# Order of the rest copies, the place of the low-rank load, the length of a warm-up bridge and the turn of the output operands in a one-core encoder block

## The chip, the cores and the metric

The kernel runs on one core of a Trainium2 chip. It is measured by the device time of one execution in microseconds (us). Three runs of the kernel before took 904.07, 904.47 and 905.79 us, with a median of 904.47. One further execution was recorded by the profiler.

## The reference

One encoder layer on 512 tokens of width 2048 in float32. A conditioning vector gives shift, scale and gate; the normalised and modulated input h is projected to all inputs of two mixers, dilated window attention (16 heads of 64, three patterns) and gated linear attention (GLA, 4 heads, whose decay comes from a low-rank product). Both results are gated, joined and projected out.

```python
    mod = jax.nn.silu(c) @ w_cond[layer] + b_cond[layer]
    shift, scale, gate = jnp.split(mod, 3, axis=-1)
    h = rms_norm(x) * (1.0 + scale[:, None]) + shift[:, None]
    proj = h @ w_in[layer]
    aq, ak, av, ag, gq, gk, gv, gg, lr_f, lr_b = jnp.split(proj, PROJ_SPLITS, axis=-1)
    ...
        o_p, lse_p = dilated_window_attention(aq, ak, av, rel_bias, window, dilation)
    ...
    mix_w = jax.nn.softmax(jnp.stack(lses, axis=0), axis=0)
    att = jnp.einsum('pbsh,pbshe->bshe', mix_w.astype(av.dtype), jnp.stack(outs, axis=0))
    a_out = att.reshape(B, S, ATT_WIDTH) * jax.nn.silu(ag)
    ...
    log_g_f = (jax.nn.log_sigmoid((lr_f @ gla_gate_up_fwd[layer] + gla_gate_bias_fwd[layer]).astype(jnp.float32))
               / GLA_GATE_NORM).reshape(ks_)
    ...
    o_bwd = jnp.flip(gla_chunked(jnp.flip(gq, 1), jnp.flip(gk, 1), jnp.flip(gv, 1),
                                 jnp.flip(log_g_b, 1)), 1)
    g_o = rms_norm(o_fwd + o_bwd).reshape(B, S, GLA_WIDTH) * gla_norm_gain[layer]
    g_out = g_o * jax.nn.silu(gg)
    y = jnp.concatenate([a_out, g_out], axis=-1) @ w_out[layer]
    x = x + gate[:, None] * y
return rms_norm(x) * final_gain
```

## The kernel before

Every large product keeps float32 accuracy by splitting both sides into a high and a low part: three() (L229) issues high by high, low by high and high by low, three matmuls of 512 columns. Weights arrive by DMA as raw tiles of 512 KB; ScalarE (ACT) copies the high part (split_hi, L493), VectorE (DVE) subtracts it to leave the low part (split_lo, L477). Each of the two takes about a microsecond and works a few groups ahead of the matmuls.

The stages follow one another on TensorE (PE), whose order is the order of the program text. First come the conditioning row, the normalisation and the first projections (sta and stb, up to about 96 us). Then the units qk2, qk4, qk6 and gk, each of 64 ticks; a tick is one three(). Attention runs beside these four units, four heads in each, from about 200 to 444 us: a side item, such as the scores of a tile, has a place between 0 and 1 of its unit and is put in at that tick. Then comes the V unit with 112 ticks, which makes the GLA values by seven Strassen products, with the low-rank product at ticks 9 to 24 and GLA head 0 beside it. The units ag0, ag1, gg0 and gg1 make the gates. Last, from about 744 us, stands the output product: seven Strassen products (in the order P1, P7, P6, P4, P5, P3, P2) for each of two pairs of row blocks, four weight groups (O0 to O55) per product, each group 12 matmuls of PE or about 2.7 us. The tail after PE's last matmul normalises and stores.

On the other engines and on the DMA queue of SyncE (SP) a scheduler orders the instructions from the place at which they were written and from what they need; each engine and each queue then runs strictly in that order, so an instruction that waits holds up what stands behind it. In a few marked regions the text's own order holds.

**Bridge.** At the start PE has nothing to multiply until the first activations are normalised. warm(n) (L293) issues n products of a constant tile hot into a bank that nobody reads: five at the very start, then, after the products that spread the conditioning row (L299), six more (L324).

**Attention of one head.** Scores s (L839, L840) for four query tiles go through a bias with a running sum on DVE (L847, in parts of 160 and 256 columns), an exponential on ACT (L851), a reciprocal on DVE (L854) and a scaling on GpSimd (POOL, L864). PE transposes the probabilities to t (L882); ACT copies the high part to pth (L888), DVE subtracts to leave ptl (L889). What is left of the first tile, one 128 x 128 block r, is transposed once (L899) and spread over four places of the two tiles by rest(): four copies of 32 x 128 on ACT (L906) and four subtractions on DVE (L908), in two pairs: two copies, their two subtractions, then the other two of each. The value product o (L915, L917) then needs all of pth and ptl. S in the orders below is a partial sum for the Strassen operands, made on the side.

**Low rank.** lrb, 256 KB of low-rank weights, is loaded on SP's queue after the gk unit has been written (L1303), in the same ring of tiles as other work; ACT and DVE split it to lrs (L1306, L1307), used by low_rank at tick 9 of V. upr (loaded at L1320) is split to ups at place 0.2 of V.

**GLA head 0.** GLA_FIRST (L122) gives the places of ten items in the V unit; the eighth and ninth, outs(0) and outs(1), are the products go (L1123), which need the decay-masked scores at (L1106, L1108 on DVE).

**Output operands.** Each Strassen product has its own operand made of blocks of cat (the joined mixer results): A11, S3, S2, A22, S1, S4 and A12, in halves z = 0 and 1. to_s1 (L1471), to_s2 (L1474) and to_s4 (L1477) form sums in place on DVE, 1.2 us each; halves() splits into a high (ACT, L1458) and a low tile (DVE, L1459). P6 uses S2, P4 uses A22, P5 uses S1 and P3 uses S4. These makings hang on a list by pair, product and group (later), and product() issues them when it writes that group, right after the lower split of the group's first weight tile; the last to_s1 and to_s2 stand before the output product, after the eviction of gg1 (L1202).

Of the kernel before, what the change touches and what calls it, by code (L numbers as in the profile page):

```python
# [10 lines left out]
F32 = mybir.dt.float32  # L11
# [109 lines left out]
GLA_AT = (0.01, 0.02, 0.33, 0.46, 0.46, 0.56, 0.64, 0.76, 0.76, 0.88)  # L121
GLA_FIRST = (0.3, 0.38, 0.55, 0.62, 0.775, 0.81, 0.86, 0.9, 0.92, 0.97)  # L122

# [68 lines left out]
def block_kernel(ctx: ExitStack, tc: tile.TileContext, a: dict):  # L192
# [108 lines left out]
    with tc.manual_schedule(engines=PLANNED):  # L301
# [18 lines left out]
        for j in range(4):  # L320
            spread(j, ch, True)
            spread(j, cl, False)
            act(sb[:, 512 * j:512 * j + 512], pcs[j], AF.Silu)
        warm(6)  # L324

# [492 lines left out]
    def attention(pairs):  # L818
# [77 lines left out]
        def rest(h):  # L896

            pk = PJ(f"r{h}")
            nc.tensor.transpose(pk[:, :P], pr_.pop((h, 0))[:, 0:128], ident)  # L899
            hi, lo = pts  # L900
            to = [(hi, 0, hi, 32), (hi, 0, lo, 0), (hi, 96, lo, 96), (hi, 64, hi, 96)]
            parts = [(t[a:a + 32, REST_OF[i], :], u[b:b + 32, REST_OF[i], :], pk[96 - 32 * i:128 - 32 * i, :P])
                     for i, (t, a, u, b) in enumerate(to)]
            for pair in (parts[:2], parts[2:]):
                for up, _, of in pair:
                    act(up, of, AF.Copy)  # L906
                for up, low_, of in pair:
                    tt(low_, of, up.bitcast(F32), op=ALU.subtract)  # L908

# [383 lines left out]

    ps = unit("gk", False, attention((6, 7)))
    kp_.close()
# [5 lines left out]

    lrb = T2("lrb")
    nc.sync.dma_start(lrb.rearrange("p (k c) -> p k c", k=KT), a["w_lr"][0])  # L1303
    lrs = gp.tile([P, KT, 2, 32], F32R, tag="g", name="lrs")
    lrb3 = lrb.rearrange("p (k c) -> p k c", k=KT)
    act(lrs[:, :, 0, :], lrb3, AF.Copy)  # L1306
# [176 lines left out]
    gate_evict(ps, cat[3], "g1")  # L1483
    to_s1(1)
    to_s2(1)
    mid.close()
# [147 lines left out]
    def later(pair, prod, g, go):  # L1634
        todo.setdefault((pair, prod, g), []).append(go)

    def product(pair, prod, ps, first, last, rows=(0, 1)):

# [25 lines left out]
    def a12():  # L1664
        operand("A12", [B8(f"A12{e}", [4, 512], F32R) for e in "hl"])

    for z in range(2):
        later(0, "P1", 2 * z, halves("S2", z, part(z, 0)))
        later(0, "P7", 2 * z, halves("A22", z, part(2 + z, 1)))
        later(0, "P6", 2 * z, halves("S1", z, part(z, 1)))  # L1670
        later(0, "P6", 2 * z + 1, lambda z=z: (to_s4(z), halves("S4", z, part(z, 0))()))
    later(0, "P4", 0, a12)
# [135 lines left out]
```

## Time and profile before

| | |
|---|---|
| runs | 904.07, 904.47, 905.79 us |
| profiled execution, its own time | 907.22 us |
| its span in the trace | 905.4 us |
| ACT, busy share | 54% |
| POOL, busy share | 14% |
| mean DMA rate | 268 GB/s |
| HBM read, written | 224.64 MB, 51.47 MB |

A profile row of the timeline has the start from the span's beginning in us, the duration, the engine, the source line, the operation, written tile <- read tiles, its shape and count, and in brackets the idle time ahead of it with what ended it. PEld are weight loads, which lie beside PE's matmuls; a row of PE ends later than the next begins, as matmuls are pipelined, so the distance between starts says more than the durations. SPq rows are DMA issues. The groups that the change touches, from the list of the costliest groups (busy us, mean ns of one, idle time ahead and its main releaser behind the bars):

```profile
L888 ACT ACTIVATE pth<-t 128x384 fp32r<-128x384 f32 x64 | 31.0, 485 | 19.8 <-PE t L882 11.1
L889 DVE TENSOR_TENSOR ptl<-t,pth 128x384 fp32r<-128x384 f32 x64 | 35.2, 551 | 5.2 <-ACT pth L888 3.7
L906 ACT ACTIVATE pth<-r 32x128 fp32r<-32x128 f32 x64 | 17.2, 269 | 9.9 <-PE r L899 4.5
L915 PE MATMUL o<-pth,vv 128*128 128x512 f32 (+1 forms) x64 | 15.9, 369 | 2.2 <-DVE pth L908 1.1
```

### The profile page before, as it was taken

What the parts mean: (1) busy time and instruction counts of PE and PEld (TensorE: products, weight loads), DVE (VectorE), ACT (ScalarE), POOL (GpSimd) and SP (SyncE); (2) the same over time, 40 slices, a digit from 0 to 9 for tenths busy, and PEclk for the clock granted to TensorE, in tenths of its full rate; (3) what the DMA queues carried; (4) which work ended last, traced back from release to release, by engine and by line L of the source; (5) the groups of instructions that cost most, each with busy time, mean ns of one, the idle gap of its engine ahead of it and who ended that gap; (6) DMA issues with size and microseconds to landing.
All of it is one profiled execution on the core that took longest, in us unless ns stands there. A gap on an engine that the chain in (4) does not pass through costs nothing.

```text
span 905.4 us, 12339 instructions
## 1 busy us (share of the span) xinstructions
PE 890.0 (98%) x4159; PEld 739.2 (82%) x4159; DVE 731.2 (81%) x1220; ACT 491.6 (54%) x841; POOL 125.9 (14%) x219
## 2 busy tenths in 40 slices
PE   8999999999999999999999999999999999999996
PEld 6888788888888888887778888888888888888885
DVE  7998799878989989888568668595787559797687
ACT  5554533466655745655657554373664248455454
POOL 0000000023323333243000101112020100000001
PEclk9999999999999999999999999999999999999999
DMA  9999489398798898998778879778796988777863
GB/s 342 401 411 363 186 344 367 134 306 226 202 266 273 247 265 247 249 298 223 232 260 255 311 206 308 206 249 262 231 279 208 275 286 289 282 288 249 289 238 154
DMA packets 65547, 242.33 MB, mean 268 GB/s; under 512 B 9190, under 2 KB 11526, under 8 KB 55883
## 3 DMA queue, kind: packets, MB, share of 16 engines
q1 hardware_dynamic: 58724, 199.23, 61.5%
q0 software_dynamic: 6464, 42.01, 19.4%
q8 instruction: 33, 0.54, 0.2%
q10 hardware_dynamic: 296, 0.30, 0.1%
q14 instruction: 30, 0.25, 0.1%
HBM read 224.64 MB, written 51.47 MB: 305 GB/s over the span
## 4 chain that ended last, share of the span: by engine, by line
PE 91%; DVE 3%; ACT 2%; DMA 2%; issue 1%; SPq 0%; DVEq 0%; ACTq 0%
PE ps_qk L230 5%; PE ps_qk L232 5%; PE ps_qk L231 5%; PE g L232 4%; PE g L230 4%; PE g L231 4%; PE stb L232 3%; PE stb L231 3%; PE stb L230 3%; PE ps_ag L232 3%; PE ps_ag L230 3%; PE ps_ag L231 3%; PE o L915 3%; PE sta L230 3%; PE sta L231 3%; PE sta L232 3%
## 5 line engine op out<-in xcount | busy, mean ns | idle before, releaser
L864 POOL TENSOR_SCALAR p<-p,st 128x32 f32<-128x32 f32 (+2 forms) x108 | 59.8, 565 | 159.9 <-DVE st L854 91.2
L328 DVE CUSTOM_DVE_ANT_0 cb<-cb,sb,c_bcond 128x2048 f32<-128x2048 f32 (+1 forms) x32 | 73.4, 2295 | 1.9 <-DMA cb<-in_wm 1.6
L851 ACT ACTIVATE p<-p,st 128x416 f32<-128x416 f32 x64 | 41.0, 641 | 49.2 <-DVE st L847 42.3
L429 POOL DMA_DIRECT2D T<-in_w_o x32 | 23.2, 725 | 159.4 <-ACT V2h L493 14.8
L888 ACT ACTIVATE pth<-t 128x384 fp32r<-128x384 f32 x64 | 31.0, 485 | 19.8 <-PE t L882 11.1
L889 DVE TENSOR_TENSOR ptl<-t,pth 128x384 fp32r<-128x384 f32 x64 | 35.2, 551 | 5.2 <-ACT pth L888 3.7
L882 PE MATMUL t<-c_ident,p 128*128 128x128 f32 x192 | 31.3, 272 | 0.0
L882 PEld LDWEIGHTS t<-c_ident,p 128*128 128x128 f32 x192 | 24.3, 139 | 7.9
L847 DVE CUSTOM_DVE_ANT_0 p<-s,g,st 128x256 f32<-128x256 f32 x64 | 27.7, 432 | 1.8
L847 DVE CUSTOM_DVE_ANT_0 p<-s,g 128x160 f32<-128x160 f32 x64 | 23.5, 367 | 4.2 <-PE s L840 3.5
L328 DVE CUSTOM_DVE_ANT_0 rawg<-rawg,crow,gate 128x1024 f32<-128x1024 f32 x16 | 20.4, 1279 | 4.0 <-DMA rawg<-in_wg 4.0
L1581 POOL TENSOR_SCALAR x<-x,rn 128x512 f32<-128x512 f32 x2 | 2.3, 1167 | 148.5 <-ACT rn L1570 148.5
L429 POOL DMA_DIRECT2D T3V<-in_w_gv x8 | 5.5, 687 | 125.1 <-ACT qk21h L493 118.7
L839 PE MATMUL s<-ks,qh 128*128 128x416 f32 x64 | 22.6, 353 | 0.0
L906 ACT ACTIVATE pth<-r 32x128 fp32r<-32x128 f32 x64 | 17.2, 269 | 9.9 <-PE r L899 4.5
L840 PE MATMUL s<-ks,ql 128*128 128x416 f32 x64 | 22.4, 350 | 0.0
L1091 ACT ACTIVATE sq<-st,sc 128x256 f32<-128x256 f32 x24 | 12.2, 506 | 18.6 <-DVE st L1081 10.0
L328 DVE CUSTOM_DVE_ANT_0 rawg<-rawg,crow,c_bcond 128x1024 f32<-128x1024 f32 x16 | 20.3, 1279 | 0.5 <-DVE g L1028 0.5
L429 POOL DMA_DIRECT2D T<-T x16 | 9.1, 571 | 79.9 <-ACT V8h L493 12.9
L915 PE MATMUL o<-pth,vv 128*128 128x512 f32 (+1 forms) x64 | 15.9, 369 | 2.2 <-DVE pth L908 1.1
L466 DVE TENSOR_TENSOR raw_O<-raw_O,raw_P 128x1024 f32<-128x1024 f32 x8 | 9.8, 1225 | 10.1 <-DMA raw_O<-in_w_o 7.8
L568 ACT ACTIVATE h_hi<-xt,shift 128x512 fp32r<-128x512 f32 x16 | 11.5, 721 | 10.3 <-DVE shift L328 9.5
(1661 smaller groups left out, 3151.6 us busy)
## 6 DMA issues: line engine op xcount, KB each, us to landing
cb<-in_wm SPq DMA_DIRECT2D x31, 1024.0 KB, 9.3
T<-in_w_o POOLq DMA_DIRECT2D x32, 512.0 KB, 6.5
rawg<-in_wg SPq DMA_DIRECT2D x32, 512.0 KB, 5.4
raw_O<-in_w_o SPq DMA_DIRECT2D x32, 512.0 KB, 4.6
raw_qk<-in_w_qk SPq DMA_DIRECT2D x24, 512.0 KB, 4.9
raw_O<-T SPq DMA_DIRECT2D x24, 512.0 KB, 5.0
rawb<-in_w_sb SPq DMA_DIRECT2D x16, 512.0 KB, 8.9
rawv<-in_wv SPq DMA_DIRECT2D x16, 512.0 KB, 5.6
```

The lines of the kernel that those rows point to most:

```text
L230: mm(ps, lh, rh, start=first, stop=False, skip_group_check=more)
L231: mm(ps, ll, rh, start=False, stop=False, skip_group_check=more)
L232: mm(ps, lh, rl, start=False, stop=last, skip_group_check=more)
L328: return nc.vector.tensor_tensor_reduce(out=w, in0=w, in1=with_, op0=ALU.mult, op1=ALU.add, scale=1.0, scalar=init, accum_out=dst)
L429: move = nc.gpsimd.dma_start(dst, src, max_dma_last_dim=8192, **how).ins
L847: top = nc.vector.tensor_tensor_reduce(out=t[:, lo:hi], in0=ps[:, lo:hi], in1=gt[h][:, at:at + 2 * (hi - lo) - 1:2], op0=ALU.add, op1=ALU.min,
L851: act(t, t, AF.Exp, bias=st[:, 0:1], scale=-1.0, accum_out=st[:, 1:2])
L864: last["pool"] = nc.gpsimd.tensor_scalar(to, of, st[:, 2:3], 1.0, op0=ALU.mult, op1=ALU.mult).ins
L882: nc.tensor.transpose(pk[:, n_ * P:n_ * P + P], t[:, first_ + kt * P:first_ + kt * P + P], ident)
L888: act(hi, src, AF.Copy)
L889: tt(lo, src, hi.bitcast(F32), op=ALU.subtract)
L915: mm(po[:, P * a0:P * a1], vv[h // 4][:, c, h % 4, :], pt[:, at:at + (a1 - a0 - 1) * step + 1:step, :], start=n_ == z == 0, stop=False, sk ...
```

## The change

Five edits. The second call of warm makes thirteen products. Two places of GLA_FIRST go up by 0.01, one tick each. rest() issues its four copies first and then its four subtractions. The load of lrb becomes a side item of the gk unit at place 0.7. The last to_s1 and to_s2 and the halves of S2, A22, S1 and S4 are issued through a new helper, in_turn, which orders them behind the last upper and lower weight splits written so far; to_s1(1) and to_s2(1) go to groups 2 and 3 of P1, and the halves of S2 to group 1 of P1 and of P7.

```diff
@@ -119,7 +119,7 @@
 TOKENS = [slice(256 * c + a, 256 * c + 256, 2) for a in range(2) for c in range(2)]
 
 GLA_AT = (0.01, 0.02, 0.33, 0.46, 0.46, 0.56, 0.64, 0.76, 0.76, 0.88)
-GLA_FIRST = (0.3, 0.38, 0.55, 0.62, 0.775, 0.81, 0.86, 0.9, 0.92, 0.97)
+GLA_FIRST = (0.3, 0.38, 0.55, 0.62, 0.775, 0.81, 0.86, 0.91, 0.93, 0.97)
 
 SUMS_IN = {"ag0": 8, "ag1": 8, "gg0": 8}
 
@@ -321,7 +321,7 @@
             spread(j, ch, True)
             spread(j, cl, False)
             act(sb[:, 512 * j:512 * j + 512], pcs[j], AF.Silu)
-        warm(6)
+        warm(13)
 
     def cond_sum(dst, w, with_, init):
 
@@ -901,11 +901,10 @@
             to = [(hi, 0, hi, 32), (hi, 0, lo, 0), (hi, 96, lo, 96), (hi, 64, hi, 96)]
             parts = [(t[a:a + 32, REST_OF[i], :], u[b:b + 32, REST_OF[i], :], pk[96 - 32 * i:128 - 32 * i, :P])
                      for i, (t, a, u, b) in enumerate(to)]
-            for pair in (parts[:2], parts[2:]):
-                for up, _, of in pair:
-                    act(up, of, AF.Copy)
-                for up, low_, of in pair:
-                    tt(low_, of, up.bitcast(F32), op=ALU.subtract)
+            for up, _, of in parts:
+                act(up, of, AF.Copy)
+            for up, low_, of in parts:
+                tt(low_, of, up.bitcast(F32), op=ALU.subtract)
 
         def values(h):
             def go():
@@ -1291,7 +1290,13 @@
         for q in range(2):
             qk_evict(p + 2 + q, ps[2 * q], ps[2 * q + 1])
 
-    ps = unit("gk", False, attention((6, 7)))
+    lrb = []
+
+    def lr_load():
+        lrb.append(T2("lrb"))
+        nc.sync.dma_start(lrb[0].rearrange("p (k c) -> p k c", k=KT), a["w_lr"][0])
+
+    ps = unit("gk", False, attention((6, 7)) + [(0.7, lr_load)])
     kp_.close()
     gs = mid.enter_context(tc.tile_pool(name="gs", bufs=1, reuse_waits="tile"))
     gla["k"] = B8("gkt", [4, 512])
@@ -1299,10 +1304,8 @@
         act(gla["k"][:, i, :], ps[i], AF.Copy)
 
 
-    lrb = T2("lrb")
-    nc.sync.dma_start(lrb.rearrange("p (k c) -> p k c", k=KT), a["w_lr"][0])
     lrs = gp.tile([P, KT, 2, 32], F32R, tag="g", name="lrs")
-    lrb3 = lrb.rearrange("p (k c) -> p k c", k=KT)
+    lrb3 = lrb[0].rearrange("p (k c) -> p k c", k=KT)
     act(lrs[:, :, 0, :], lrb3, AF.Copy)
     tt(lrs[:, :, 1, :], lrb3, lrs[:, :, 0, :].bitcast(F32), op=ALU.subtract)
     plr = PA("plr")
@@ -1481,8 +1484,6 @@
             (0.65, lambda: to_s1(0)), (0.8, lambda: to_s2(0))]
     ps = unit("gg1", False, side + some_sums("gg1"))
     gate_evict(ps, cat[3], "g1")
-    to_s1(1)
-    to_s2(1)
     mid.close()
     op = ctx.enter_context(tc.tile_pool(name="op", bufs=1, reuse_waits="tile"))
     for e in "hl":
@@ -1633,6 +1634,14 @@
 
     def later(pair, prod, g, go):
         todo.setdefault((pair, prod, g), []).append(go)
+
+    def in_turn(pair, prod, g, *fns):
+
+        def go():
+            with tc.issue_after(last["hi"]), tc.issue_after(last["lo"]):
+                for fn in fns:
+                    fn()
+        later(pair, prod, g, go)
 
     def product(pair, prod, ps, first, last, rows=(0, 1)):
 
@@ -1664,11 +1673,13 @@
     def a12():
         operand("A12", [B8(f"A12{e}", [4, 512], F32R) for e in "hl"])
 
+    in_turn(0, "P1", 2, lambda: to_s1(1))
+    in_turn(0, "P1", 3, lambda: to_s2(1))
     for z in range(2):
-        later(0, "P1", 2 * z, halves("S2", z, part(z, 0)))
-        later(0, "P7", 2 * z, halves("A22", z, part(2 + z, 1)))
-        later(0, "P6", 2 * z, halves("S1", z, part(z, 1)))
-        later(0, "P6", 2 * z + 1, lambda z=z: (to_s4(z), halves("S4", z, part(z, 0))()))
+        in_turn(0, ("P1", "P7")[z], 1, halves("S2", z, part(z, 0)))
+        in_turn(0, "P7", 2 * z, halves("A22", z, part(2 + z, 1)))
+        in_turn(0, "P6", 2 * z, halves("S1", z, part(z, 1)))
+        in_turn(0, "P6", 2 * z + 1, lambda z=z: to_s4(z), halves("S4", z, part(z, 0)))
     later(0, "P4", 0, a12)
     for z in range(2):
         later(0, "P4", 1 + 2 * z, lambda z=z: halves("A12", z, part(2 + z, 0))())
```

Since the scheduler places the work anew, the order on the engines shows more than the diff. Behind an arrow stand the tiles read; numbers behind tile names tell buffers apart, and an ISA row of L847 is the score bias with its sum.

First place, DVE at head 13, before: the rest subtractions are L908, the weight split of the gk unit is gk7l, and the last row is the next tile's bias (the second row of each L847, which reads the sum out, is left out).

```order
733 L908 TENSOR_TENSOR pth<-r_4040,pth 32x128
734 L908 TENSOR_TENSOR ptl<-r_4040,pth 32x128
735 L889 TENSOR_TENSOR ptl<-t_4050,pth 128x3x128
736 L847 ISA p_4063,st_4064<-s_4060,g_3867 128x160
738 L477 TENSOR_TENSOR gk7l<-raw_gk_3978,gk7h 128x1024
739 L847 ISA p_4063,st_4064<-s_4060,g_3867,st_4064 128x256
741 L908 TENSOR_TENSOR ptl<-r_4040,pth 32x128
742 L1243 TENSOR_TENSOR S_4001<-S_4001,h_lo 128x512
743 L908 TENSOR_TENSOR pth<-r_4040,pth 32x128
744 L854 RECIPROCAL st_4064<-st_4064 128x1
745 L847 ISA p_4095,st_4096<-s_4092,g_3867 128x256
```

The same place after, where the rest subtractions are L907:

```order
727 L907 TENSOR_TENSOR pth<-r_4047,pth 32x128
728 L847 ISA p_4070,st_4071<-s_4067,g_3874 128x160
730 L907 TENSOR_TENSOR ptl<-r_4047,pth 32x128
731 L847 ISA p_4070,st_4071<-s_4067,g_3874,st_4071 128x256
733 L907 TENSOR_TENSOR ptl<-r_4047,pth 32x128
734 L1242 TENSOR_TENSOR S_4008<-S_4008,h_lo 128x512
735 L907 TENSOR_TENSOR pth<-r_4047,pth 32x128
736 L854 RECIPROCAL st_4071<-st_4071 128x1
737 L889 TENSOR_TENSOR ptl<-t_4057,pth 128x3x128
738 L847 ISA p_4102,st_4103<-s_4099,g_3874 128x256
740 L477 TENSOR_TENSOR gk7l<-raw_gk_3985,gk7h 128x1024
```

Weight split and L889 both stood between the subtractions; now all four subtractions come ahead of them, and the next tile's bias (row 738 after, 745 before) has L889 ahead of it, with the split behind.

Second place, ACT around head 15, before: the exponential of the head's first tile is row 362, the copy of the low-rank weights row 382, and the rest copies are L906.

```order
360 L888 ACTIVATE pth<-t_4129 128x3x128
361 L493 ACTIVATE V0h<-raw_V_4076 128x1024
362 L851 ACTIVATE p_4143,st_4144<-p_4143,st_4144 128x416
363 L888 ACTIVATE pth<-t_4162 128x3x128
364 L906 ACTIVATE pth<-r_4188 32x128 x2
380 L888 ACTIVATE pth<-t_4286 128x3x128
381 L906 ACTIVATE pth<-r_4296 32x128 x2
382 L1306 ACTIVATE lrs<-lrb 128x16x32
383 L888 ACTIVATE pth<-t_4306 128x3x128
384 L906 ACTIVATE pth<-r_4296 32x128 x2
```

After, with the rest copies as L905:

```order
346 L888 ACTIVATE pth<-t_4138 128x3x128
347 L1309 ACTIVATE lrs<-lrb 128x16x32
348 L851 ACTIVATE p_4152,st_4153<-p_4152,st_4153 128x416
349 L888 ACTIVATE pth<-t_4171 128x3x128
350 L493 ACTIVATE V0h<-raw_V_4083 128x1024
351 L905 ACTIVATE pth<-r_4197 32x128 x4
365 L1329 ACTIVATE ups<-upr 128x1024
366 L888 ACTIVATE pth<-t_4295 128x3x128
367 L1304 ACTIVATE gkt<-ps_gk_3679 128x512
368 L905 ACTIVATE pth<-r_4305 32x128 x4
369 L888 ACTIVATE pth<-t_4315 128x3x128
```

The copy lrs left the place between the rest copies at the head's end and stands ahead of the exponential of its first tile; the exponential also moved ahead of the split V0h, and the copy ups now stands between the head's last tiles. On SP's queue the load lrb moved from behind the seventh V load to behind the fifth.

Third place, DVE at the beginning of the output product, before: L1202 is the last gate's eviction, L1477 and L1471 are sums of operands, O2l and O3l lower weight splits.

```order
1058 L1459 TENSOR_TENSOR c_l<-cat_1611,c_h 128x1024
1059 L1202 TENSOR_TENSOR cat_5990<-cat_5990,sgg_6783 128x512
1060 L1477 TENSOR_TENSOR cat_1611<-cat_5127,cat_1611 128x4x256
1061 L1471 TENSOR_TENSOR cat_3027<-cat_5990,cat_3027 128x4x256
1062 L477 TENSOR_TENSOR O2l<-raw_O_6807,O2h 128x1024
1063 L1474 SCALAR_TENSOR_TENSOR cat_3027<-cat_3027 128x4x256
1064 L477 TENSOR_TENSOR O3l<-raw_O_6809,O3h 128x1024
1065 L477 TENSOR_TENSOR O4l<-raw_O_6811,O4h 128x1024
```

After, where the eviction is L1201, the sums are L1474 (to_s1) and L1477 (to_s2), and L1462 is the lower half of an operand:

```order
1050 L1201 TENSOR_TENSOR cat_5997<-cat_5997,sgg_6790 128x512
1051 L477 TENSOR_TENSOR O2l<-raw_O_6812,O2h 128x1024
1052 L1462 TENSOR_TENSOR c_l<-cat_1618,c_h 128x1024
1053 L1474 TENSOR_TENSOR cat_3034<-cat_5997,cat_3034 128x4x256
1054 L477 TENSOR_TENSOR O3l<-raw_O_6814,O3h 128x1024
1055 L1477 SCALAR_TENSOR_TENSOR cat_3034<-cat_3034 128x4x256
1056 L477 TENSOR_TENSOR O4l<-raw_O_6816,O4h 128x1024
1057 L477 TENSOR_TENSOR O5l<-raw_O_6818,O5h 128x1024
```

The split O2l now comes right behind the eviction, ahead of the sums.

## The prediction

> **What bounds the kernel.** I read the page first: busy time by engine, then the chain that ended last, followed back from the last instruction.
>
> ```profile
> span 905.4 us, 12339 instructions
> ...
> PE 890.0 (98%) x4159; PEld 739.2 (82%) x4159; DVE 731.2 (81%) x1220; ACT 491.6 (54%) x841; POOL 125.9 (14%) x219
> ...
> PE 91%; DVE 3%; ACT 2%; DMA 2%; issue 1%; SPq 0%; DVEq 0%; ACTq 0%
> ```
>
> PE is busy 890.0 of 905.4 us and holds 91% of the chain. The change takes no multiplication away (it adds seven), so it can only fill holes between matmuls or end a time in which they run slowly. The next view is the list of PE's waits.
>
> ```profile
> PE sta L591 <- ACT h_hi L534: 2.7, 1, 2.7
> ...
> PE o L915 <- DVE pth L908: 1.1, 1, 1.1
> PE o L915 <- ACT pth L888: 1.0, 1, 1.0
> PE go L1123 <- ACT V27h L493: 0.3, 1, 0.3
> ```
>
> The columns are total, times and longest. The first stands at the start, as does the one left out, for the first bridge's tile. The next two, at L915, are the attention value products of head 13 and head 15; the last is a GLA product in the V stage. Few targets are left: this list without the start is 2.4 us. The rest is found by going along PE's timeline and comparing the start of each matmul with its predecessor's; a 512-column step is 0.23 us. Measured so, the holes that the change speaks of are 1.27 us at head 13 (418.32), 1.17 at head 15 (442.31), 0.26 at head 1, 0.18 at head 9, 0.13 just before head 4, 0.44 at the GLA product and 0.30 in the output product: 3.75 us, worked out from starts like those quoted below.
>
> **Thirteen bridging products.** The start on PE, then the same stretch in windows (length, then PE busy, PEld, DVE, ACT, POOL, the granted clock, DMA share, GB/s):
>
> ```profile
> 6.08 1.52 PE L296 MATMUL warm<-hot 128*128 128x512 f32 x6
> 10.25 1.21 PE L591 MATMUL sta<-sa0hi,h_hi 128*128 128x512 f32 x4 [2.65 <-ACT h_hi L534]
> 11.28 1.90 PE L591 MATMUL sta<-sa0lo,h_hi 128*128 128x512 f32 x4
> ```
> ```profile
> 7.87:11.28 3.41, 1.03 (x5) 0.84 (x6) 2.81 (x6) 2.23 (x5) 0.00 (x0) 1.00 1.03 407
> 11.28:14.69 3.41, 3.41 (x10) 2.64 (x9) 2.31 (x3) 1.00 (x2) 0.00 (x0) 0.50 1.03 429
> 895.30:898.70 3.40, 1.62 (x8) 1.00 (x6) 2.29 (x6) 2.23 (x7) 0.99 (x1) 1.00 0.24 95
> 898.70:902.10 3.40, 0.00 (x0) 0.00 (x0) 2.14 (x5) 2.05 (x6) 0.00 (x0) 1.00 0.77 308
> ```
>
> After a 3.41 us stretch with PE busy for 1.03 (30%) the clock is 0.50 for the next 3.41; four products then take 1.90 instead of 1.21 with their pipeline, about 0.42 a step instead of 0.23. Eight such steps fit: 8 x 0.20 = 1.6 us. A stretch with 1.62 busy (48%, at 895.30) was still followed by a clock of 1.00. Seven more products at 0.23 carry the bridge from 7.60 to about 9.2, so that stretch would hold 2.6 of 3.41 (77%), above the 48% that cost nothing. The products write a bank of their own and finish a microsecond before h_hi is ready at 10.25, so they lie inside the idle 2.65 us. Worth: -1.6 against the profiled execution.
>
> **Against the median** this counts differently. The profiled execution took 907.22 us by its own clock, the runs 904.07, 904.47 and 905.79. The highest lies 1.3 to 1.7 above the others, about the price of one half-clock stretch. I read it so: such stretches have a fixed beat that a run meets by chance, the two lower runs did not pay, the highest and the profiled one did. Of 907.22 - 904.47 = 2.75 us, 1.6 would be this and 1.1 the profiling.
>
> **Rests: four copies, then four subtractions.** Head 13, the dearest case:
>
> ```profile
> 413.14 0.57 ACT L906 ACTIVATE pth<-r 32x128 fp32r<-32x128 f32 x2
> 413.74 0.29 DVE L908 TENSOR_TENSOR pth<-r,pth 32x128 fp32r<-32x128 f32 x1 [0.17 <-ACT pth L906]
> 414.05 0.28 DVE L908 TENSOR_TENSOR ptl<-r,pth 32x128 fp32r<-32x128 f32 x1
> 414.12 1.05 ACT L493 ACTIVATE gk7h<-raw_gk 128x1024 fp32r<-128x1024 f32 x1
> 414.84 0.31 DVE L847 CUSTOM_DVE_ANT_0 p<-s,g 128x160 f32<-128x160 f32 x1
> 415.20 1.22 DVE L477 TENSOR_TENSOR gk7l<-raw_gk,gk7h 128x1024 fp32r<-128x1024 f32 x1
> 416.35 0.48 DVE L847 CUSTOM_DVE_ANT_0 p<-s,g,st 128x256 f32<-128x256 f32 x1
> 416.86 0.29 DVE L908 TENSOR_TENSOR ptl<-r,pth 32x128 fp32r<-32x128 f32 x1
> 417.17 0.69 DVE L1243 TENSOR_TENSOR S<-S,h_lo 128x512 f32<-128x512 f32 x1
> 417.89 0.28 DVE L908 TENSOR_TENSOR pth<-r,pth 32x128 fp32r<-32x128 f32 x1
> 418.32 1.05 PE L915 MATMUL o<-pth,vv 128*128 128x512 f32 x4 [1.10 <-DVE pth L908]
> ```
>
> ACT puts a 1.05 us weight split (gk7h) between the two pairs, and DVE follows with its own 1.22 (gk7l); the last subtraction ends at 418.17, 5.03 us after the first copy. Now all four copies go first (4 x 0.29 = 1.16 us) and the first subtraction starts 0.57 later than today. By the new DVE order there follow pth 0.31, L847 0.36, ptl 0.31, L847 0.51, ptl 0.31, S 0.72, pth 0.28: 1.17 + 2.80 = 3.97 us. So the last ends 1.06 earlier, which bounds the gain at head 13. Against it stands what the split displaced: L889 (0.48 from start to start) and the reciprocal now stand between this head's last subtraction and the next head's L847, so each chain can start up to about 0.5 later. Gain between 0.5 and 1.06; I take **-0.8**.
>
> The other heads had no split in their way, or less:
>
> ```profile
> 226.87 0.28 DVE L908 TENSOR_TENSOR pth<-r,pth 32x128 fp32r<-32x128 f32 x1
> 227.30 1.06 PE L915 MATMUL o<-pth,vv 128*128 128x512 f32 x4
> ```
>
> The last subtraction of head 1 ends 0.15 before the value product, which is the hand-over itself: no reserve, and head 9 reads alike. At head 1 the chain takes 3.94 today, 3.97 by the new order, and what is shifted by 0.5 ahead of it arrives in full. Heads 0, 4 and 5 have 0.27 to 0.38 by the same reading, the even heads 2, 6, 10 and 14 over 1.2. All together between 0 and +1.2; I take **+0.4**, one head's shift.
>
> **The low-rank weights.** Today, at the end of gk, and the place to which the copy moves:
>
> ```profile
> 434.49 0.64 SPq L1303 DMA_DIRECT2D lrb<-in_w_lr  x1
> 441.12 0.63 ACT L1306 ACTIVATE lrs<-lrb 128x512 fp32r<-128x512 f32 x1 [2.78 <-DMA lrb<-in_w_lr]
> 442.31 1.13 PE L915 MATMUL o<-pth,vv 128*128 128x512 f32 x4 [1.01 <-ACT pth L888]
> ```
> ```profile
> 424.79 0.63 ACT L851 ACTIVATE p<-p,st 128x416 f32<-128x416 f32 x1
> 427.66 0.38 DVE L847 CUSTOM_DVE_ANT_0 p<-s,g,st 128x160 f32<-128x160 f32 x1
> 429.31 0.49 PE L882 MATMUL t<-c_ident,p 128*128 128x128 f32 x3
> ```
>
> The profile names pth L888, but ACT stood 2.78 us at the lrs copy for the load, and L888 and the last rest copies were queued behind it. That stall (1.17) goes, since lrs leaves this place. But lrs does not merely become early: it now stands ahead of the exponential of head 15's first tile (424.79), and behind lrs on ACT wait that exponential, L888, V0h and the four rest copies; on DVE, behind its own lrs half, L889, V0l and the second tile's L847 (427.66), whose score bank the transposes at 429.31 reuse. From landing L: lrs 0.63, exponential 0.83, reciprocal 0.16, DVE lrs 0.69, L889 0.48, L847 0.45, V0l 1.2, L847 0.4: L + 4.85. With PE 0.8 earlier, the transposes are due at 428.5, so L has to be 423.7 or less.
>
> When does it land? On SP's queue the load stands right behind the fifth V load, which waits for the buffer that gk7l frees. gk7l ends today at 416.4; in the new order (L889, L847, then gk7l) at about 419.3. So lrb is issued near 419.6. It took 6.6 us from 434.49 to 441.1; two rows bound it otherwise, first this stretch's 512 KB loads, then all loads of that line (minimum, median, maximum):
>
> ```profile
> raw_V<-in_w_gv SPq DMA_DIRECT2D x3, 512.0 KB, 4.6
> ```
> ```profile
> DMA to landing us min/median/max: 3.1/4.8/10.0
> ```
>
> With 3.1 it lands at 422.7 and nothing stalls; with 4.6 at 424.2 (stall 0.5); with 6.6 at 426.2 (stall 2.5). I take 5.4, between its own time and the loads around it: stall 1.3, less 1.17: **+0.1**, between -1.2 and +1.4.
>
> The copy ups moves as well, from behind head 15's rests into its last chain:
>
> ```profile
> 443.36 1.05 ACT L1326 ACTIVATE ups<-upr 128x1024 fp32r<-128x1024 f32 x1
> ```
>
> Without the wait for lrb, ACT was free at 441.12 - 2.78 = 438.34; L888 and the last rest copies would end near 439.4 and DVE's last subtraction near 440.3, 0.8 ahead of the value product's due time of 442.31 - 1.17 = 441.1. A copy of 1.05 within that chain takes the 0.8 and 0.25 more if nothing hides it: 0 to +0.3; I take **+0.2**.
>
> **Two GLA outputs a tick later, and the output operands.**
>
> ```profile
> 524.30 0.69 DVE L1108 SCALAR_TENSOR_TENSOR at<-c_ident,at 128x512 f32<-128x512 f32 x1
> 525.13 0.46 PE L1123 MATMUL go<-at,gv 128*128 128x128 f32 x2 [0.28 <-ACT V27h L493]
> ```
> ```profile
> 748.88 1.22 DVE L477 TENSOR_TENSOR O2l<-raw_O,O2h 128x1024 fp32r<-128x1024 f32 x1
> 750.15 0.50 PE L232 MATMUL g<-O2l,A11h 128*128 128x512 f32 x1
> ```
>
> The first GLA product lacks DVE's mask (524.30 to 524.98), 0.44 us late; V27h, named as releaser, is not its operand. One tick is three matmuls, 0.68 us, more than the hole: **-0.4** (0 to -0.44, as the second output follows at the old distance). O2l starts at 748.88, behind two 1.2 us sums; now it stands ahead of them, and the product at 750.15 needs no wait: **-0.3**. What is late next there are the operands S2 and S1: they move by one to three groups, and the eight groups from O0 to O7, 2.7 us each, still end 10 us after the last sum's new place. The remaining side work of DVE fits between its splits; I cost it at 0 and at +0.5 if it does not.
>
> **The sum.** Against the profiled execution: -1.6 - 0.8 + 0.4 + 0.1 + 0.2 - 0.4 - 0.3 = -2.4, so 904.8 of 907.22 by its own clock, less 1.1 for profiling: **903.7**. Against the median the bridge counts nothing, and -0.8 gives the same 903.7.
>
> **Rivals.**
> - *Every hole closes* (the load lands by 423.7, the shift is absorbed by DVE's idle time): 904.47 - 3.75 = 900.7. For it: DVE is busy 81%, and each head has short idle times; against it: heads 1 and 9 have 0.15 in reserve.
> - *The clock still halves.* If a run's half-clock stretch has another cause than the 2.65 us of idle, thirteen products buy nothing, and a median that pays gives 903.7 + 1.6 = 905.3. Against it: the half stretch starts exactly one 3.41 us beat after the 30% one.
> - *The load lands late and stops head 15 earlier* (slower). Behind the fifth V load and beside the sixth, it could take the 10.0 of the row above: L = 429.6, a stall of 5.9 in place of 1.17, 904.47 - 0.9 + 4.7 = 908.3. It decides from L = 425.8 on (slower than before), and by over 0.2% from about 427.6, a flight of 8.0 us.
>
> [...]
>
> **How the numbers follow.** A measurement of this kernel can tell about 0.2%, 1.8 us, from no change: faster is below 902.7, slower above 906.3. Forecast 0.50, all holes close 0.22, the clock 0.14, the late load 0.14. Faster: 0.22 and 0.13 of the forecast's 0.50 (rests at their better bounds, an early load): 0.35. Slower: most of the late load, 0.11. The rest is same, 0.54. The range 901.0 to 905.8 takes in the forecast's bounds (-1.2 and +1.4 at the load, 0 to +1.2 at the rests, 0.8 above or below in combination) and most of the first two rivals; the late load is left out.
>
> **What would show it.** The changed profile should have no clock under 1.00 between 5 and 15 us; a value product of head 13 with under 0.8 us of idle; no ACT idle before lrs near 441, but one before head 15's first exponential, with the transposes after it late by L + 4.85; no hole at O2l; the GLA product in step. A first value product at heads 1 and 9 without a larger hole would refute the shift; a lrb flight under 4 us or over 8 would make the prediction wrong.

## The result, and the profile after

The change makes the kernel slower: 907.08 us (median of 22 runs, 906.0 to 909.41) against 904.86 (22 runs, 903.95 to 908.57), a ratio of 1.0023 with an interval of 1.0016 to 1.0029. The prediction was 903.7, within 901.0 to 905.8. The profiled execution after took 909.41 us by its own clock, the slowest of its 22.

The page of the changed kernel, its span and the busy shares:

```profile
span 907.6 us, 12330 instructions
...
PE 894.1 (99%) x4166; PEld 741.2 (82%) x4166; DVE 730.0 (80%) x1220; ACT 491.6 (54%) x841; POOL 125.0 (14%) x219
```

PE is still the bound. The waits of PE (total, times, longest) say where the new holes are:

```profile
PE s L839 <- DVE ptl L889: 1.8, 1, 1.8
PE warm L296 <- DVE hot L308: 1.5, 1, 1.5
PE s L839 <- DVE st L847: 0.8, 3, 0.3
PE t L882 <- DVE st L847: 0.5, 1, 0.5
PE ps_gv_P L232 <- DVE V21l L477: 0.2, 1, 0.2
```

Every wait that the change aimed at has left the list: the value products (L915 before, L914 after), the GLA product, the idle time ahead of sta. By the starts a hole of 0.19 us stays at head 13's value product. In their place PE waits at the scores (s) and the transposes (t) of attention, where it had not waited before, but for 0.13 just before head 4. The largest, 1.8 us, is at head 15.

Timeline rows around it, on DVE, SP's queue, ACT and PE, in this order:

```profile
418.55 1.27 DVE L477 TENSOR_TENSOR gk7l<-raw_gk,gk7h 128x1024 fp32r<-128x1024 f32 x1
419.88 0.33 SPq L391 DMA_DIRECT2D raw_V<-in_w_gv  x1
420.31 0.47 SPq L1297 DMA_DIRECT2D lrb<-in_w_lr  x1
427.07 0.63 ACT L1309 ACTIVATE lrs<-lrb 128x512 fp32r<-128x512 f32 x1 [4.99 <-DMA lrb<-in_w_lr]
427.60 0.63 ACT L851 ACTIVATE p<-p,st 128x416 f32<-128x416 f32 x1
429.02 0.55 DVE L889 TENSOR_TENSOR ptl<-t,pth 128x384 fp32r<-128x384 f32 x1
429.63 0.46 PE L839 MATMUL s<-ks,qh 128*128 128x416 f32 x1 [1.76 <-DVE ptl L889]
431.50 0.88 PE L882 MATMUL t<-c_ident,p 128*128 128x128 f32 x3 [0.54 <-DVE st L847]
```

Read downwards, this is one chain. gk7l ends at about 419.8 and frees a buffer; the fifth V load goes out at 419.88, lrb right behind it at 420.31; it lands 6.7 us later; ACT has stood idle for 4.99 us at lrs, with head 15's first exponential behind it; DVE's L889 comes at 429.02; and PE, which had reached the scores at 427.70 (the preceding product starts at 427.47), goes on at 429.63. A second hole of 0.70 follows at the transposes.

Then comes something that no wait shows. Windows of one clock beat each (length, PE busy, PEld, DVE, ACT, POOL, granted clock, DMA share, GB/s):

```profile
427.57:430.98 3.41, 1.63 (x7) 0.86 (x5) 2.63 (x7) 3.29 (x10) 0.97 (x1) 1.00 0.08 31
430.98:434.39 3.41, 2.89 (x9) 2.36 (x9) 3.21 (x14) 1.08 (x3) 1.75 (x4) 0.50 0.63 223
```

In the beat behind the hole the clock is halved, to 0.50. Products that follow at 0.43 instead of 0.23 add 1.4 us here. The kernel before had its half stretch at 11.28, behind the idle time ahead of sta; in this execution there is none at the start.

### The profile page after: what moved, and what is told of

It is laid out like the page before. It is cut to its first block, busy times and chain, and to the rows that moved or that the text cites. A ratio compares the mean times of both kernels' runs of the same rounds, so it can differ in the third digit from the quotient of the medians.

```text
span 907.6 us, 12330 instructions
## 1 busy us (share of the span) xinstructions
PE 894.1 (99%) x4166; PEld 741.2 (82%) x4166; DVE 730.0 (80%) x1220; ACT 491.6 (54%) x841; POOL 125.0 (14%) x219
## 4 chain that ended last, share of the span: by engine, by line
PE 47%; DVE 3%; DMA 2%; ACT 2%; issue 1%; DVEq 0%; SPq 0%; ACTq 0%
PE g L232 4%; PE g L230 4%; PE g L231 4%; PE ps_ag L230 3%; PE ps_ag L232 3%; PE ps_ag L231 3%; PE ps_gg L230 2%; PE ps_gg L231 2%; PE ps_gg L232 2%; PE ps_gv_P L232 2%; PE ps_gv_P L231 2%; PE ps_gv_P L230 2%; PE go L1122 2%; PE gx L231 2%; PE gx L230 2%; PE gx L232 2%
## 5 line engine op out<-in xcount | busy, mean ns | idle before, releaser
L889 DVE TENSOR_TENSOR ptl<-t,pth 128x384 fp32r<-128x384 f32 x64 | 34.9, 549 | 3.1 <-ACT pth L888 2.3
L847 DVE CUSTOM_DVE_ANT_0 p<-s,g,st 128x256 f32<-128x256 f32 x64 | 27.6, 432 | 1.7
L847 DVE CUSTOM_DVE_ANT_0 p<-s,g 128x160 f32<-128x160 f32 x64 | 23.6, 369 | 4.5 <-PE s L840 3.8
L905 ACT ACTIVATE pth<-r 32x128 fp32r<-32x128 f32 x64 | 17.2, 268 | 5.0 <-PE r L899 3.7
L839 PEld LDWEIGHTS s<-ks,qh 128*128 128x128 f32 x64 | 12.0, 188 | 8.5 <-PE ps_qk L232 2.3
L854 DVE RECIPROCAL st<-st 128x1 f32<-128x1 f32 x64 | 10.2, 159 | 10.1 <-ACT p L851 9.5
L1358 DVE TENSOR_TENSOR vS<-rawS,vS 128x1024 fp32r<-128x1024 f32 x8 | 9.7, 1223 | 9.6 <-ACT vS L1357 9.5
```

The costliest lines, as they stand in the source:

```text
L839: mm(ps[:, :NK], qh[:, q], ks[:, k], start=True, stop=False)
L847: top = nc.vector.tensor_tensor_reduce(out=t[:, lo:hi], in0=ps[:, lo:hi], in1=gt[h][:, at:at + 2 * (hi - lo) - 1:2], op0=ALU.add, op1=ALU.min,
L889: tt(lo, src, hi.bitcast(F32), op=ALU.subtract)
```

## The experiments

All ratios stand against runs of the kernel before on the same chip; "before" is their median. Intervals are 95%.

| run | edit | us | before | ratio (interval) |
|---|---|---|---|---|
| change | all five edits | 907.08 | 904.86 | 1.0023 (1.0016 to 1.0029) |
| e1_late_load | change, load of lrb put back | 904.84 | 905.36 | 0.9995 (0.9986 to 1.0004) |
| e2_pairs | change, rests put back | 904.12 | 905.36 | 0.9987 (0.9978 to 0.9996) |
| e3_late_pairs | change, both put back | 903.80 | 905.36 | 0.9986 (0.9977 to 0.9995) |
| e4_bridge | before, thirteen products | 905.73 | 905.36 | 1.0004 (0.9995 to 1.0013) |
| e5_early | change, load at 0.5 | 905.41 | 904.86 | 1.0005 (0.9996 to 1.0014) |
| e6_four_at_13 | e3, four and four at head 13 | 902.98 | 904.86 | 0.9980 (0.9971 to 0.9989) |
| e7_four_but_13 | change, pairs at head 13 | 906.55 | 904.86 | 1.0018 (1.0009 to 1.0027) |
| e8_no_bridge | before, no second bridge | 908.27 | 904.86 | 1.0033 (1.0020 to 1.0046) |
| e9_change_again | the change | 906.67 | 905.14 | 1.0016 (1.0007 to 1.0025) |
| e10_best_six | e6, six products | 903.78 | 905.14 | 0.9982 (0.9972 to 0.9992) |
| e11_best_early | e6, load at 0.5 | 902.55 | 905.14 | 0.9972 (0.9961 to 0.9983) |
| e12_before_again | before, once more | 905.19 | 904.39 | one run each |

### Load and rests, each put back and both

e1 on the change, the load back behind the unit:

```diff
-    ps = unit("gk", False, attention((6, 7)) + [(0.7, lr_load)])
+    ps = unit("gk", False, attention((6, 7)))
...
+    lr_load()
     lrs = gp.tile([P, KT, 2, 32], F32R, tag="g", name="lrs")
```

e2 on the change, the rests in pairs; e3 has both edits:

```diff
-            for up, _, of in parts:
-                act(up, of, AF.Copy)
-            for up, low_, of in parts:
-                tt(low_, of, up.bitcast(F32), op=ALU.subtract)
+            for pair in (parts[:2], parts[2:]):
+                for up, _, of in pair:
+                    act(up, of, AF.Copy)
+                for up, low_, of in pair:
+                    tt(low_, of, up.bitcast(F32), op=ALU.subtract)
```

> The changed kernel with only the load of lrb put back behind the gk unit; the four copies of the rests stay first. Load theory: the 2.63 us of PE waiting at head 15's second tile (1.93 and 0.70) and the half-clock stretch behind it (about 1.4) go, the 1.07 that head 15's end had won is lost only if lrs lands between the rest copies again, which by the new order it does not; so about 3 to 4 us less than the change, 903.0 to 904.0, under the kernel before. Rest theory (the four-and-four order is what costs): the time stays at 906 or more, since every rest is unchanged.

> The changed kernel with only the rests put back to two and two; the load stays beside gk. Load theory: the stall at head 15's first tiles stays (ACT waits some 5 us for lrb, PE 2 to 3 us, perhaps a half-clock stretch), time 905.5 to 907. Rest theory: the 1.9 us that PE lost between head 0 and head 13 (-1.47 to +0.46 against before) goes, and the time falls to about 905 with 1.2 us of hole at head 13 back.

> Both put back: what is left of the change is the bridge of thirteen, the two GLA places and the turn of the operands. If these three are worth what their holes were (0.44 and 0.30, and the bridge between 0 and 1.5 in a median), the time is 0.7 to 2.2 us under before, 902.6 to 904.1; if the holes move elsewhere (the profile of the change has a new 0.36 at V21l), it is within 0.4 of before.

Only the third came as expected: e1 is about a microsecond over its range, and e2 has no stall at all where one was expected. Against the kernel before, e3 is 1.6 us faster; the late load with the new rests (e1) loses 1.0 of that; the load beside gk with the old rests (e2) loses 0.3; both together, the change, are 1.5 to 2.2 us slower than before, so they lose 3.1 to 3.8. **Alone the two edits cost 1.0 and 0.3 us; another 1.7 to 2.4 come only when they meet.** Each of the ratios behind these differences has an interval of about 0.8 us to either side, so the sizes are rough. The traces say the same: the holes at head 15 are 2.0 to 2.6 us in the change, 0.13 in e1, and 0.12 and 0.27 in e2. Why is seen in e2, DVE, SP's queue and ACT:

```profile
413.29 1.22 DVE L477 TENSOR_TENSOR gk7l<-raw_gk,gk7h 128x1024 fp32r<-128x1024 f32 x1
416.40 0.51 SPq L1298 DMA_DIRECT2D lrb<-in_w_lr  x1
422.98 0.63 ACT L1310 ACTIVATE lrs<-lrb 128x512 fp32r<-128x512 f32 x1 [2.31 <-DMA lrb<-in_w_lr]
```

With pairs, gk7l starts at 413.29 in e2 and the fifth V load went out right behind it, so lrb is issued at 416.40 (a store of S stands between the two there), four microseconds ahead of the change. It takes 6.5 us, as long as in the change, and lands early enough, ahead of the 423.7 that the prediction asked for, that PE's holes at head 15's scores are 0.12 at most, with one of 0.27 later in that head. The four-and-four order had pushed gk7l back, gk7l holds the V load, and the V load holds lrb.

The late load has next to no hole at head 15 either (0.13): in e1 the copy left the place between the rest copies for the V stage, and ACT reached it at 440.4, when lrb had just landed.

### The load by itself: early, and with head 13 left out

e5 on the change:

```diff
-    ps = unit("gk", False, attention((6, 7)) + [(0.7, lr_load)])
+    ps = unit("gk", False, attention((6, 7)) + [(0.5, lr_load)])
```

e7 on the change, around the same loops as in e2:

```diff
+            for pair in ((parts,) if h != 13 else (parts[:2], parts[2:])):
```

> The changed kernel with the load of lrb at place 0.5 of gk in place of 0.7: on SP's queue it now stands ahead of the three V loads, so the buffer that the split gk7l frees no longer holds it, while ACT's copy lrs stays at the same place ahead of head 15's first exponential. Queue theory (lrb is late because gk7l, moved back by the rests, holds the fifth V load ahead of it): lrb lands some 10 us earlier, ACT's idle 5.0 us before lrs and PE's 1.93 and 0.70 go, time 903.5 to 904.8, as with the late load. Rival (the copy's place on ACT and DVE costs in itself, or the four-and-four rests do): 906 or more.

> The changed kernel (load at 0.7) with pairs at head 13 and four and four at all others. gk7l then stands behind the last rest subtraction of head 13, and the load behind it. Queue theory: what lrb costs goes by when gk7l ends; if it ends near 417 as with pairs throughout, lrb lands by 424 and PE waits under 0.7 at head 15; the 1.9 us at the other heads' scores stay, head 13's hole is 1.2 again, time about 905 to 906. Rival (any four-and-four order makes the load late): 907 as the change.

e5 keeps lrs on ACT ahead of head 15's first exponential (one instruction earlier than in the change, with the split V0h back between the two) and moves the load ahead of the V loads on the queue:

```profile
405.67 0.49 SPq L1297 DMA_DIRECT2D lrb<-in_w_lr  x1
421.14 0.62 ACT L1309 ACTIVATE lrs<-lrb 128x512 fp32r<-128x512 f32 x1
```

ACT does not wait at all, PE's largest hole at head 15 is 0.43, and 1.0 to 1.7 us of the change's loss are back (1.0005 against 1.0016 and 1.0023). So most of the cost is the landing. The time was 0.6 over the range expected, and most of what stays is the rests: e1 has the same rests and lies at 0.9995. The 0.9 us by which e5 is above e1 are within the two intervals; the hole of 0.43, against 0.13 in e1, may be the copy's place. In e7 gk7l ended near 419.0, not 417 as expected, lrb went out at 419.46 and landed near 424.5, and PE's holes at head 15 were 0.24, 0.16 and 1.20. Head 13's hole was 0.59, not 1.2 as expected. The time, 906.55, is over the 905 to 906 of the queue theory, but head 15's holes rank by when lrb is issued (at 416.40, in e2, 0.27; at 419.46 1.6 us; at 420.31, in the change, 2.6 us), as that theory has it. With the other heads' rests in fours, gk7l stands behind head 13's last rest subtraction and is late even where head 13 keeps its pairs.

### Head 13 alone

e6 on e3:

```diff
-            for pair in (parts[:2], parts[2:]):
+            for pair in ((parts,) if h == 13 else (parts[:2], parts[2:])):
```

> Four copies and four subtractions at head 13 alone, two and two at the other heads, the load of lrb behind gk; bridge, GLA places and operands as in the change. If the four-and-four order helps only where a weight split stood between its pairs: head 13's hole falls from 1.26 to about 0.3 and no hole opens at the scores of other heads, 0.9 to 1.0 us under the version with pairs throughout, 902.6 to 903.1. If the 1.9 us lost among the heads came from head 13 itself or from the rest of the change: 904 to 905.

902.98, as expected. The times alone do not show the 0.9 to 1.0 us between e6 and the version with pairs, though: each against its own runs of before, e6 is 1.9 under and e3 1.6, a difference within the noise. The rest is read from the starts. On DVE and PE of e6:

```profile
413.80 0.29 DVE L908 TENSOR_TENSOR pth<-r,pth 32x128 fp32r<-32x128 f32 x1 [0.76 <-ACT pth L906]
417.08 1.44 DVE L477 TENSOR_TENSOR gk7l<-raw_gk,gk7h 128x1024 fp32r<-128x1024 f32 x1
415.74 0.42 PE L839 MATMUL s<-ks,qh 128*128 128x416 f32 x1
416.89 0.97 PE L915 MATMUL o<-pth,vv 128*128 128x512 f32 x4
```

The value product has no hole (1.27 before); the scores ahead of it have one of 0.30. That one is head 13's own: it stands in the change and in e6, and not in e7, where head 13 alone keeps its pairs. The other heads keep their small holes of before (0.22, 0.13, 0.19) and get no new ones. So head 13 gains 1.0 us net in e6 (the prediction took 0.8); most of the loss belongs to other heads.

What the fours cost there shows at head 1 in the change, on DVE and PE:

```profile
223.37 0.29 DVE L907 TENSOR_TENSOR pth<-r,pth 32x128 fp32r<-32x128 f32 x1 [1.01 <-ACT pth L905]
223.69 0.33 DVE L847 CUSTOM_DVE_ANT_0 p<-s,g 128x160 f32<-128x160 f32 x1
224.38 0.48 DVE L847 CUSTOM_DVE_ANT_0 p<-s,g,st 128x256 f32<-128x256 f32 x1
225.01 0.43 PE L839 MATMUL s<-ks,qh 128*128 128x416 f32 x1
```

DVE stands idle for 1.01 us until the fourth copy is done (at 223.34), since the first subtraction is at the head of its queue. Behind it stands the bias of the next head's tile, L847; its score bank is read out at 224.86, and the next scores on PE, which write into a freed bank, start at 225.01, 0.25 late. Holes of this kind stand behind the rests of heads 0, 1, 4, 6, 10 and 13: 0.20, 0.25, 0.44 (0.13 of it there before), 0.14, 0.44 and 0.41 (e9: 0.20, 0.19, 0.44, 0.14, 0.45, 0.43). The other ten heads open none.

### The change and the kernel before, once more

> The changed kernel unaltered, for a second profile and beside the next two on one chip. If lrb's lateness and PE's wait for it belong to the order and not to one execution: lrb issued near 420, landing 4.5 to 7 us later, a hole of 0.5 to 2.7 us at head 15's second tile, some 2 us slower than before. The half-clock stretch of 3.41 us behind the hole may or may not show again: it depends on how the beat falls on the hole (the trace before needs some 2 us of idle within one stretch).

> The kernel before unaltered, for a second profile. Which of its holes belong to the order and which to one execution: if set by the order on ACT and DVE, head 13's hole is 1.27 again within 0.05, as are 0.44 at the GLA product and 0.30 at O2l; if set by a load's landing, head 15's hole (1.17) may lie anywhere from 0 to 1.5. The half-clock stretch at the start comes if about 2 us of idle fall into one stretch of the beat, otherwise not; without it the execution should lie near 904.9 instead of 907.2.

Both profiled executions are free of half-clock stretches while PE works, which makes them the better pair. The change again:

```profile
420.09 0.45 SPq L1297 DMA_DIRECT2D lrb<-in_w_lr  x1
425.05 0.63 ACT L1309 ACTIVATE lrs<-lrb 128x512 fp32r<-128x512 f32 x1 [3.19 <-DMA lrb<-in_w_lr]
429.48 0.52 PE L882 MATMUL t<-c_ident,p 128*128 128x128 f32 x3 [0.52 <-DVE st L847]
432.43 0.43 PE L839 MATMUL s<-ks,qh 128*128 128x416 f32 x1 [1.03 <-DVE st L847]
```

The load took 4.9 us this time instead of 6.7, and the holes at head 15 came to 0.14, 0.69 and 1.20: 2.0 us against 2.6. The waits of the kernel before, second profile:

```profile
PE sta L591 <- ACT h_hi L534: 1.2, 1, 1.2
PE o L915 <- DVE pth L908: 1.1, 1, 1.1
PE o L915 <- ACT pth L888: 0.8, 1, 0.8
PE go L1123 <- ACT V27h L493: 0.3, 1, 0.3
```

Head 13's hole is 1.27 again, the GLA product's 0.45, O2l's 0.30: these belong to the order. Head 15's is 0.93 (1.17 in the first, 1.03 in e8, none in e4): it goes with the load. Starts of the same product on PE, e9 less e12, give the balance:

| from, to | change |
|---|---|
| first projection (sta) starts, with h_hi, which is ready at 10.11 and 9.60 | +0.52 |
| up to the last scores ahead of head 13's value product | +1.92 |
| head 13's value product | -0.99 |
| head 15's first tiles | +2.17 |
| end of head 15, to its value product | -0.83 |
| V21l (a hole of 0.26 in e12, none in e9) | -0.45 |
| GLA outputs, output operands | -0.92 |
| last product of PE | +1.42 |

By their own clocks the two executions took 906.63 and 905.19, 1.44 apart. Of the +1.92, 0.42 is the hole at the scores that is head 13's own, so the other heads lost 1.5 and head 13 gained 0.57 net. In the first profile of the change head 15's first tiles took 4.06 instead of 2.17, of which 1.4 are the half-clock stretch.

### The bridge

e4 on the kernel before (e8 has warm(0) there, and e10 is e6 with warm(6)):

```diff
-        warm(6)
+        warm(13)
```

> The kernel before with thirteen bridging products and nothing else. By the beat of the clock windows as the traces show it (a 3.41 us stretch with 30% or 38% of PE busy is followed by a halved one, with 46% not), a run of before pays 1.6 us when about 2 us of the 2.65 us of idle fall into one stretch, in some two runs of three; thirteen then save about 1.0 us in the mean: ratio 0.9985 to 0.9992. Rival (2.65 us of idle never halves the clock): no difference, ratio 0.9998 to 1.0002.

> The kernel before without the second bridge (no product between the spread products and the first projection). The idle time of PE grows from 2.65 to over 4 us, so every run should pay a half-clock stretch of 1.6 us. If the median of before mostly does not pay: 1.0 to 1.6 slower, ratio 1.0011 to 1.0018. If it mostly pays already: under 0.5, ratio up to 1.0005.

> The version with four and four at head 13 only and the late load, with six bridging products instead of thirteen. If the bridge is worth something in a median, it is 0.5 to 1.5 us slower than with thirteen (903.0 beside a before of 904.9, so 903.5 to 904.5); if it is worth nothing, as the bridge alone showed (ratio 1.0004, 0.9995 to 1.0013): within 0.4 of 1.9 us under before.

e4 has no measurable difference: its time lies on the rival's side, though the rival's reason does not hold, as the first profile of before has the halved clock behind 2.65 us of idle. e10, 1.4 us under before by the medians and 1.6 by the ratio against 1.9 and 1.8 for e6, shows no difference either. e8, without any bridge, is 3.4 us slower by the medians (five runs; 3.0 by the ratio, interval 1.8 to 4.2), more than the 1.6 of one half stretch. Its idle time ahead of sta was 2.90 us, not over 4, and its profile shows one half stretch. By the starts this execution, 908.27 and so 3.1 slower than e12, lost 0.6 because h_hi was ready later (10.23 against 9.60), 1.5 in the half stretch and 1.1 at small holes from 791 us on, of which the largest is 0.33 at O43l. Whether the other four runs lost the same stays open. The beats of e8 and of the second profile of before:

```profile
7.08:10.49 3.41, 0.51 (x3) 0.21 (x2) 2.79 (x7) 2.25 (x5) 0.00 (x0) 1.00 1.00 372
10.49:13.91 3.42, 3.42 (x9) 2.65 (x9) 2.46 (x3) 1.62 (x4) 0.00 (x0) 0.50 1.02 420
```
```profile
6.46:9.88 3.41, 2.20 (x10) 1.54 (x9) 2.88 (x7) 2.41 (x5) 0.00 (x0) 1.00 0.99 370
9.88:13.29 3.41, 3.41 (x16) 2.76 (x16) 2.98 (x3) 1.81 (x4) 0.00 (x0) 1.00 1.02 418
```

With six products the first profile of before paid and the second did not: there sta waits 1.21 us, not 2.65, and 2.20 of the beat are busy. e10 did not pay either (a wait of 1.37, 2.04 busy). Besides on h_hi, the wait depends on when the products at the start go from steps of 0.43 us to steps of 0.23: near 4.5 us from the start of the span in the first profile of before, 6.5 in the second, 7.4 in e10. In these three the bridge whose steps shorten later also ends later (its last row at 7.60, 8.44 and 8.89), and the idle time behind it is 2.65, 1.21 and 1.37 (sta starts at 10.25, 9.65 and 10.26). So the stretch in the profile that the prediction started from was a chance event of that execution, and the median of before mostly does not contain it. None of the ten profiles with thirteen products has such a stretch, and one of the three with six has; that the seven products prevent it is argued from the beat, not shown.

Nor are the seven products always free. In e4 the steps change near 7.8 us:

```profile
7.33 3.34 PE L296 MATMUL warm<-hot 128*128 128x512 f32 x13
10.51 1.07 PE L591 MATMUL sta<-sa0hi,h_hi 128*128 128x512 f32 x4
9.11 0.53 ACT L534 ACTIVATE h_hi<-xt,scale 128x256 fp32r<-128x256 f32 x1 [0.42 <-DVE scale L328]
```

h_hi is ready at 9.64 and PE comes to sta at 10.51, straight from the bridge, about 0.8 us late. In the first profile of the change it is 9.80 and 10.49, 0.6 late; in e5 0.3, and in the other seven profiles with thirteen 0.1 at most. How gain and cost weigh in a median the runs do not part.

### A version that beats both

e11 on e6, with the late lr_load() taken out again:

```diff
-    ps = unit("gk", False, attention((6, 7)))
+    ps = unit("gk", False, attention((6, 7)) + [(0.5, lr_load)])
```

> Four and four at head 13 only, with the load at place 0.5 of gk instead of after it. Queue theory: lrb lands before its copy is due, ACT's copy ahead of head 15's first exponential costs its own 0.63 alone, PE's wait at head 15 is at most 0.4 us, time within 0.5 of the version with the late load, 1.4 to 2.2 us under before. Rival (an lrs copy within head 15's chain costs by itself): 1 us or more above the late load.

902.55 us, 0.9972 (0.9961 to 0.9983): 2.6 us under the kernel before and 4.1 under the change (e9) on the same chip. SP's queue, and the waits of PE that are left:

```profile
404.23 0.49 SPq L1298 DMA_DIRECT2D lrb<-in_w_lr  x1
```
```profile
PE warm L296 <- DVE hot L308: 1.5, 1, 1.5
PE sta L591 <- ACT h_hi L534: 0.4, 1, 0.4
PE sta L231 <- DVE h_lo L537: 0.2, 1, 0.2
```

None of this list is left behind the start. By the starts 0.31 remains at the scores that head 13's rest holds up. The gap to the late load (e6) is within what these runs can tell.

## Why the prediction was wrong, point by point

- **The load of lrb** was booked at +0.1 (a stall of 1.3 against 1.17 won). The chain was right: the queue, gk7l's end (419.3 expected, 419.8 and 419.6 measured), lrs ahead of the exponential, what stands behind it. The size was wrong. Issued at 420.1 to 420.3 instead of 419.6 and landing at 425.05 and 427.07 instead of 425.0, it cost 2.2 us in one profile and 4.1 in the other, and 0.83 was won at the end of head 15: +1.3 to +3.2. It was not the flight: in e9 the load landed when the forecast said, and still cost 2.2 instead of 1.3. Three things were left out. PE's first stop is at the scores, which need L889, ahead of the transposes. Behind the transposes PE stops again, at the next scores: 1.20 in e9 at 432.43, against 0.43 in e5, where the load is early. And in the first profile the beat with the hole of 1.93 us at the scores was followed by one at a clock of 0.50, which added 1.4; behind e9's holes there was none. The rival of the late load, held at 0.14, has the same direction and mechanism, with a landing of 429.6 that did not come. Its decision point (L = 425.8) was too late: e9 is slower than before with 425.05, because the rests lost as well.
- **The rests** were the other wrong step: -0.4 booked, +0.9 in e9. Head 13's value product gains 0.99 (0.8 taken, bounds 0.5 to 1.06), but the scores ahead of it lose 0.42 of that to the same rest, which leaves 0.57. For the other heads +0.4 was taken between 0 and +1.2; they lost 1.5. The prediction had noted that the first subtraction slips by 0.57 and looked for the consequence at the last subtraction and the value products; it came at the bias behind the first subtraction in DVE's queue, and at the scores that wait for its bank. By the prediction's own sign the shift at the value products is refuted: the hole at head 1's went from 0.25 to 0.17 and that at head 9's from 0.18 to nothing. Heads 6 and 10, left out for their reserve of over 1.2 us at the value product, are among those that opened a hole at the scores.
- **The two together**: the prediction worked out from the new order when gk7l ends, and so when lrb leaves, but booked the cost of that lateness at next to nothing. With the rests in pairs the same place of the load costs 0.3 us (e2); with the new rests 1.7 to 2.4 more.
- **The GLA outputs and the operands** did what was said: no hole at either place, -0.92 with what lies around them against -0.7 booked.
- **The bridge** was right for the median (nothing). The mechanism agrees as far as it was seen (no half stretch at the start in any of the profiles with thirteen), but that the products lie inside the idle time and cost nothing holds only where the bridge ends ahead of h_hi: in three of the ten profiles, with the steps at the start shortening near 7.7 (the change), 7.8 (e4) and 6.8 (e5), they held up sta by 0.3 to 0.8. The bookkeeping of the profiled execution was wrong: 907.22 was not 1.1 us of profiling above the runs. Its span and its own time differ by 1.8 in each kernel, and e12's 905.19 lies among the runs; 907.22 was one long execution.
- **The copy ups** (+0.2) shows nothing: head 15's value product has no hole in the change.

## What to carry to other kernels

Two edits that cost little one by one can meet in a queue: ask of every load what it stands behind, which buffer that one waits for, and which edit moves the instruction that frees it. Where a group of copies is gathered ahead of a group of subtractions, the cost here was not at their end but at what stands behind the first of them on the waiting engine. Reorder where the hole is, here at one head of sixteen, and not in the helper that all of them call.

## What the runs showed of the hardware that was not expected

The granted clock was halved for one beat of 3.41 us behind beats in which PE was busy for 0.51, 1.03 and 1.63 us (e8, before, the change), and not behind 1.62 (before, at 895.30), 2.04 (e10), 2.20 (e12) and more. The beat of 1.63 held idle times of 1.93 and 0.17 us by the starts of its products, that of 1.62 one of 1.8 behind PE's last product, at 896.9. (By the starts alone 1.31 of the first beat are busy, the 38% of e4's expectation.) Busy time alone does not part these two, 48% of a beat each; what decides there was not tried.

In the first profile of before the clock goes to 0.50 at 11.28, back to 1.00 at 14.69 and to 0.50 again at 902.16, behind PE's last product and a beat with 0.00 busy; from 14.69 to 902.16 are 260 lengths of 3.413 us. The beats did not lie at one distance from the start of the span: those ahead of the half stretches at 11.28 and 10.49 begin at 7.87 in the first profile of before and at 7.08 in e8. The beats of e10 and e12, near 7.4 and at 6.46, are the author's estimate from where the steps at the start shorten.

ACT's exponential of head 15 had its input from 423.63 (the L847 that ended then) and started at 427.60, 3.97 us later, behind a copy that waited 4.99 us for a load. That it would stand behind that copy was in the forecast.
